# Gate and up of the feed-forward: four pairs of k-tiles of a block in seven block products for eight, and two k-tiles' residues by an accumulating DMA

## The chip, the cores and the metric

The kernel runs on one core of a Trainium2 chip. The metric is the time of one execution in device microseconds (us), the median of several runs. The core has a tensor engine (PE, with PEld for its weight loads), a vector engine (DVE), a scalar engine (ACT), GpSimd (POOL), and SyncE (SP), which here issues loads and stores. Each engine takes its own instructions in their written order.

## The reference

One residual block on 256 tokens of 2048 values, in fp32:

```python
h  = x + W_out @ [DiffAttn(xn) ; ConformerConv(xn)]     # xn = rms_norm(x) * norm1_g
hn = rms_norm(h) * norm2_g
out = h + (silu(hn @ w_gate) * (hn @ w_up)) @ w_down    # 2048 -> 5632 -> 2048
```

The change concerns the two products hn @ w_gate and hn @ w_up. Together they are 2 x 256 x 2048 x 5632 multiplications, the largest part of the block.

## The kernel before, in words

Every product with a weight keeps fp32's precision by a split: each operand is rounded to a shorter form (hi), and the residue (lo = value - hi) is kept beside it. A product is three matrix products, hi x hi, lo x hi and hi x lo, summed in PSUM. The activations' hi and lo (xhi, hhi, ahi and xlo, hlo, alo) are made once. The weights arrive in fp32 and are split as they come.

The unit of this stream is a chunk: two k-tiles of 128 rows by 512 columns of a weight, half a megabyte. `split_chunk` (L265) issues its load into `raw` (SP), has ACT round it into `whi` (L275) and DVE subtract to get `wlo` (L276). `multiply` (L289) issues the first half of its PE work, the eight products with whi (L306, L307), then the second half, the four with wlo (L312): 2 k-tiles x 2 halves of the tokens x 3 = 12 products of 128x128 by 128x512. `run_chunks` emits the split of a chunk AHEAD = 2 chunks before its products. raw has RAW_BUFS = 5 buffers, whi and wlo HL_BUFS = 4 each, so that ACT's rounding waits until PE has used an earlier chunk's whi.

Beside this stream run generators (`silu_done`, `up_done`, `out_done` and others): after each half of a chunk, `resume` lets each go on to its next `yield`, and what it emits there stands in the engines' queues at that place. Since each engine works in order, this emission order is the schedule. DVE's convolution and other filler are fed in by `run_side`.

Stages in order: the products with w_in with attention and convolution (to about 265 us), w_out (to about 360 us), then the feed-forward. Its 5632 columns are 11 blocks j of 512. For each, a gate sum (16 k-tiles, 8 chunks) and an up sum (8 chunks) for both halves of the tokens, in two of the four PSUM banks `acc` each; then silu of the gate on ACT (L713), a = up x rstd x silu on DVE (L721), four transposes on PE twice (L729), and the split of the result (L732 ACT, L733 DVE). FGROUPS = (6, 5): after six blocks, and after the last five, a pass of w_down over the blocks so far adds into h (L746, DVE). hT holds the transpose of h x norm2_g as hi and lo; the row factor rstd2 is applied only in L713 and L721.

A block has 16 chunks, 192 products and 16 transposes.

Of the kernel before, what the change touches and what calls it, by code (L numbers as in the profile page):

```python
# [38 lines left out]
# where the rows of the gains and biases begin, 128 values to a row  # L39
# [41 lines left out]
def tile_block(  # L81
# [9 lines left out]
    lhs = ctx.enter_context(tc.tile_pool(name="lhs", bufs=KD))  # L91
# [7 lines left out]
    # ---------------------------------------------------------------- inputs and constants  # L99
# [7 lines left out]
    # the tensor engine's clock rises while the first loads are under way  # L107
# [7 lines left out]
    rows = const.tile([NR, P], F32, tag="rows", name="rows")  # L115
    act.dma_start(out=rows, in_=gains)
    # a first use of the activation table before anything waits for it
# [11 lines left out]
    cw = const.tile([P, NCT, W], F32, tag="cw", name="cw")  # L129
# [15 lines left out]
    def late_constants():  # L145
# [10 lines left out]
        # q is scaled by 1/sqrt(d) through its gain  # L156
        act.mul(gb[:, 0, :], gb[:, 0, :], 1.0 / math.sqrt(DH))
        hd = DH // 2
        for i, key in enumerate("qk"):
            for m in range(NM):  # L160
                t = const.tile([P, 2, DH], F32, tag=f"gcs{key}{m}", name=f"gcs{key}{m}")
# [12 lines left out]
    def negative_lambda():  # L174
        """-lambda = exp(l2) - exp(l1) - lambda_init"""
# [5 lines left out]
    def rsqrt_mean(dst, ss, n, eps):  # L181
        """dst = (ss / n + eps) ** -0.5 on a few columns."""
# [4 lines left out]

    def lhs_pair(pfx, k):
        hi = lhs.tile([P, S], F32R, tag="lhi", name=f"{pfx}hi{k}")
        lo = lhs.tile([P, S], F32R, tag="llo", name=f"{pfx}lo{k}")  # L190
        return hi, lo

    def split_scaled(pair, src, scale):
        """hi + lo = src * scale, src in PSUM."""
# [21 lines left out]
    # banks of the aux pool that are read in a later stage than they are written  # L216
# [7 lines left out]
    # work of the vector engine that fills what the stream leaves free  # L224
# [12 lines left out]
    def side_step():  # L237
        """One step of the two oldest chains by turns: a step waits for the one before it."""
# [11 lines left out]
    def block(w, cols, ks, xs, done=None, bkey=None, first=True, last=True, spare=False, cuts=()):  # L250
        """Products of the k-tiles ks with columns of w, summed in two banks."""
# [6 lines left out]
        while i < len(ks):  # L258
# [4 lines left out]
                               done=done if i == len(ks) else None, spare=spare))  # L263

    def split_chunk(w, k0, nk, cols, width, **_):  # L265
        view = lambda t: t.rearrange("p (k n) -> p k n", n=width)[:, :nk]
        raw = view(wp.tile([P, NK * N], F32, tag="raw", name="raw", bufs=RAW_BUFS))
        o = 0
        for c, n in cols:
            sp.dma_start(out=raw[:, :, o : o + n],  # L270
                         in_=w[k0 * P : (k0 + nk) * P, c : c + n].rearrange("(k p) n -> p k n", p=P))
            o += n
        hi = view(wp.tile([P, NK * N], F32R, tag="whi", name="whi", bufs=HL_BUFS))
        lo = view(wp.tile([P, NK * N], F32R, tag="wlo", name="wlo", bufs=HL_BUFS))
        act.copy(hi, raw)  # L275
        dve.tensor_tensor(lo, raw, hi.bitcast(F32), ALU.subtract)  # L276
        spend(LO_US * nk * width / N)
        return hi, lo
# [10 lines left out]
    def multiply(c, hi, lo):  # L289
# [24 lines left out]
        if c is chunks[-1]:  # L314
            # one half of the tokens after the other, which shortens the end
# [18 lines left out]
    def run_chunks():  # L334
        ready = deque()
        n = len(chunks)
        i = 0
        for t in range(n):
            while i < min(n, t + 1 + lead(t)):
                if i in before:  # L340
                    before[i]()
                ready.append(split_chunk(**chunks[i]))
                i += 1
            multiply(chunks[t], *ready.popleft())
# [3 lines left out]
    # ---------------------------------------------------------------- x, its transpose  # L348
# [40 lines left out]
    # ---------------------------------------------------------------- convolution channels  # L389
# [7 lines left out]
    def glu_done(c0, nct, ps):  # L397
        """ps holds the gates of nct channel tiles, then what they gate."""
# [40 lines left out]
    # layer norm with tokens on partitions, and back  # L439
# [5 lines left out]
    def conv_back(b):  # L445
# [21 lines left out]
        # the table of the silu below, ahead of need  # L467
# [34 lines left out]
    # ---------------------------------------------------------------- attention  # L502
# [19 lines left out]
    def qk_rows(key, b, m, ps):  # L522
        """Norm and rotation of the heads of block b, and their transpose."""
# [32 lines left out]
    def attend_scores(hd):  # L556
# [63 lines left out]
        # in the place of the head's q, which is done with  # L620
# [48 lines left out]
    # ---------------------------------------------------------------- output projection  # L669
# [4 lines left out]
    def out_done(n, ps):  # L674
# [18 lines left out]
        if n == D // N - 1:  # L693
# [8 lines left out]
            ffn["pool"] = ctx.enter_context(tc.tile_pool(name="ffn", bufs=1))  # L702

    # ---------------------------------------------------------------- feed-forward
# [4 lines left out]
    def silu_done(ps):  # L709
        yield  # L710
        for m in range(NM):
            sil[m] = ffn["pool"].tile([P, N], F32, tag="sil", name="sil", bufs=4)
            act.activation(sil[m], ps[m], AF.Silu, scale=rstd2[m])  # L713

    def up_done(j, ps):
# [3 lines left out]
        for m in range(NM):  # L719
            a = fp.tile([P, N], F32, tag="a", name="a", bufs=4)  # L720
            dve.scalar_tensor_tensor(a, ps[m], rstd2[m], sil[m], ALU.mult, ALU.mult)  # L721
            aa.append(a)
        yield
        for t in range(N // P // 2):
# [5 lines left out]
            hi = fp.tile([P, 2, S], F32R, tag="ahi", name="ahi", bufs=FGROUPS[0] * 2)  # L730
            lo = fp.tile([P, 2, S], F32R, tag="alo", name="alo", bufs=FGROUPS[0] * 2)
            act.copy(hi, pt)  # L732
            dve.tensor_tensor(lo, pt, hi.bitcast(F32), ALU.subtract)  # L733
            for i in range(2):
                actT[j * (N // P) + 2 * t + i] = (hi[:, i, :], lo[:, i, :])
            yield

# [13 lines left out]
    # ---------------------------------------------------------------- the order of it all  # L751
# [19 lines left out]
    for g, nb in enumerate(FGROUPS):  # L771
        for j in range(j0, j0 + nb):
            block(w_gate, j * N, range(KD), fh, silu_done)
# [5 lines left out]
    lead = lambda t: 1 if t < len(XPARTS) else AHEAD  # L779
# [30 lines left out]
```

## Time and profile before

| What | Value |
|---|---|
| runs before | 1091.35, 1090.16, 1091.2 us; median 1091.2 |
| span of the profiled execution | 1089.8 us (its own time beside the span is not listed; the median is 1.4 above the span) |
| one feed-forward block (403.50 to 447.97 us) | 44.47 us |
| granted clock of TensorE, mean | 0.998 |

A row of the groups gives the line, the engine and the operation, what is written and read, the shapes and the number of instructions; behind the first bar the busy time in us and the mean ns of one; behind the second the idle time of the engine just before them and what ended it. A row of the timeline gives the start, the duration, the engine, the line and the operation, and in brackets the idle time before it. A row of the waits gives who waited for whom, the total in us, the number of times and the longest. The window rows are explained where they stand.

### The profile page before, as it was taken

The numbers are of one execution on the slowest core, as the hardware profiler recorded it, in microseconds if no ns is written. First come the engines' busy times: TensorE is split into PE (matmuls) and PEld (weight loads), VectorE is DVE, ScalarE is ACT, GpSimd is POOL, SyncE is SP. The second block draws the span as 40 slices with busy tenths as digits, with TensorE's granted clock in tenths as the row PEclk, the third lists the DMA queues.
The fourth block names the chain that finished last, engine by engine and source line by source line (L and its number), as shares of the span: only waits on it lengthen the run. The fifth ranks groups of instructions, "written<-read, shape, count | busy, mean of one in ns | idle before, by whom it ended". The sixth has DMA issues, their size and how long they took to land.

```text
span 1089.8 us, 13224 instructions
## 1 busy us (share of the span) xinstructions
PE 1079.0 (99%) x4952; PEld 894.0 (82%) x4952; DVE 647.1 (59%) x828; ACT 509.6 (47%) x719; POOL 49.1 (5%) x77
## 2 busy tenths in 40 slices
PE   8999999999999999999999999999999999999998
PEld 7988888877888888888888888888888888888886
DVE  4799989898766544544545454444454454544443
ACT  6644566755754544434444343333443444433332
POOL 0030112210100100000000000000000000000000
PEclk9999999999999999999999999999999999999999
DMA  8756665554456557666575555556666656653654
GB/s 241 233 177 198 190 189 161 154 169 155 155 181 206 174 172 220 187 192 189 168 214 184 192 192 193 192 187 190 194 186 192 189 169 211 186 192 108 219 204 146
DMA packets 118733, 203.02 MB, mean 186 GB/s; under 512 B 6932, under 2 KB 28878, under 8 KB 118668
## 3 DMA queue, kind: packets, MB, share of 16 engines
q1 hardware_dynamic: 118608, 202.14, 59.7%
q8 instruction: 39, 0.64, 0.2%
q14 instruction: 26, 0.21, 0.1%
q10 hardware_dynamic: 60, 0.03, 0.0%
HBM read 200.04 MB, written 2.10 MB: 185 GB/s over the span
## 4 chain that ended last, share of the span: by engine, by line
PE 92%; DVE 3%; ACT 2%; POOL 1%; issue 1%; DMA 1%; SPq 1%; DVEq 0%; ACTq 0%
PE acc L307 30%; PE acc L312 30%; PE acc L306 30%; DVE y L431 1%; DVE wlo L276 1%; PE ps_a L729 1%; ACT whi L275 1%; DMA h<-in_x_dram 1%; PE ps_o L643 1%; ACT junk L355 0%; POOL rsq L185 0%; PE ps_h L686 0%; SPq L360 0%; POOL fq L186 0%; SPq L270 0%
## 5 line engine op out<-in xcount | busy, mean ns | idle before, releaser
L276 DVE TENSOR_TENSOR wlo<-raw,whi 128x1024 fp32r<-128x1024 f32 (+1 forms) x377 | 456.4, 1221 | 337.3 <-ACT whi L275 304.5
L275 ACT CAST whi<-raw 128x1024 fp32r<-128x1024 f32 (+1 forms) x377 | 390.8, 1051 | 366.4 <-PE acc L307 326.6
L306 PE MATMUL acc<-whi,hhi 128*128 128x512 f32 x704 | 274.8, 390 | 0.0
L307 PE MATMUL acc<-whi,hlo 128*128 128x512 f32 x704 | 274.1, 389 | 0.0
L312 PE MATMUL acc<-wlo,hhi 128*128 128x512 f32 x704 | 189.2, 391 | 0.0
L307 PEld LDWEIGHTS acc<-whi,hlo 128*128 128x128 f32 x704 | 132.2, 188 | 27.3
L306 PEld LDWEIGHTS acc<-whi,hhi 128*128 128x128 f32 x704 | 132.2, 188 | 27.2
L312 PEld LDWEIGHTS acc<-wlo,hhi 128*128 128x128 f32 x704 | 131.4, 188 | 26.8
L306 PE MATMUL acc<-whi,ahi 128*128 128x512 f32 x384 | 150.7, 392 | 0.0
L307 PE MATMUL acc<-whi,alo 128*128 128x512 f32 x384 | 150.5, 392 | 0.0
L306 PE MATMUL acc<-whi,xhi 128*128 128x512 f32 (+1 forms) x352 | 130.0, 376 | 2.8 <-ACT xhi L196 2.8
L307 PE MATMUL acc<-whi,xlo 128*128 128x512 f32 (+1 forms) x352 | 128.6, 372 | 0.5 <-DVE xlo L197 0.4
L431 DVE SCALAR_TENSOR_TENSOR y<-upad,cw,y 128x256 f32<-128x256 f32 x240 | 103.6, 481 | 3.5 <-ACT y L424 3.0
L312 PE MATMUL acc<-wlo,ahi 128*128 128x512 f32 x384 | 103.6, 391 | 0.0
L312 PE MATMUL acc<-wlo,xhi 128*128 128x512 f32 (+1 forms) x352 | 88.7, 377 | 1.4 <-DVE wlo L276 1.2
L306 PEld LDWEIGHTS acc<-whi,ahi 128*128 128x128 f32 x384 | 72.1, 188 | 15.9
L307 PEld LDWEIGHTS acc<-whi,alo 128*128 128x128 f32 x384 | 72.1, 188 | 15.3
L312 PEld LDWEIGHTS acc<-wlo,ahi 128*128 128x128 f32 x384 | 71.9, 188 | 15.6
L306 PEld LDWEIGHTS acc<-whi,xhi 128*128 128x128 f32 x352 | 66.5, 189 | 14.7 <-ACT xhi L196 3.2
L307 PEld LDWEIGHTS acc<-whi,xlo 128*128 128x128 f32 x352 | 66.6, 189 | 11.9 <-DVE xlo L197 0.9
L312 PEld LDWEIGHTS acc<-wlo,xhi 128*128 128x128 f32 x352 | 62.3, 190 | 13.0 <-DVE wlo L276 2.2
L733 DVE TENSOR_TENSOR alo<-ps_a,ahi 128x512 fp32r<-128x512 f32 x22 | 15.2, 691 | 46.0 <-ACT ahi L732 46.0
(138 smaller groups left out, 544.2 us busy)
## 6 DMA issues: line engine op xcount, KB each, us to landing
raw<-in_w_gate_dram SPq DMA_DIRECT2D x88, 512.0 KB, 4.4
raw<-in_w_up_dram SPq DMA_DIRECT2D x88, 512.0 KB, 4.5
raw<-in_w_down_dram SPq DMA_DIRECT2D x88, 512.0 KB, 4.2
raw<-in_w_in_dram SPq DMA_DIRECT2D x48, 512.0 KB, 3.7
raw<-in_w_out_dram SPq DMA_DIRECT2D x32, 512.0 KB, 3.7
raw<-in_w_in_dram SPq DMA_DIRECT2D x62, 256.0 KB, 3.6
h<-in_x_dram SPq DMA_DIRECT2D x6, 256.0 KB, 6.1
out_dram<-h SPq DMA_DIRECT2D x6, 256.0 KB, 2.5
```

The lines of the kernel that those rows point to most:

```text
L275: act.copy(hi, raw)
L276: dve.tensor_tensor(lo, raw, hi.bitcast(F32), ALU.subtract)
L306: pe.matmul(ps[m], xhi[:, ms], hi[:, j, :], start=c["first"] and j == 0, stop=False)
L307: pe.matmul(ps[m], xlo[:, ms], hi[:, j, :], start=False, stop=False)
L312: pe.matmul(ps[m], xhi[:, ms], lo[:, j, :], start=False, stop=c["last"] and j == nk - 1)
L431: dve.scalar_tensor_tensor(y[:, ct, :], src, wk, y[:, ct, :], ALU.mult, ALU.add)
L643: pe.matmul(o[:, m, :], wT[:, (0 if m == 0 else 1 + k), :], v_sb[k][:, hd * E : (hd + 1) * E], start=k == 0, stop=k == m)
L729: pe.transpose(pt[:, i, m * P : (m + 1) * P], aa[m][:, c : c + P], ident)
L733: dve.tensor_tensor(lo, pt, hi.bitcast(F32), ALU.subtract)
```

## The change

Blocks 1 to 10 are computed by `fast_block`. The 16 k-tiles of a block form 8 pairs (k, k + 8). For the first NS = 4 pairs, up and gate, both k-tiles and both halves of the tokens make a 2 x 2 by 2 x 2 product of blocks, done with seven block products in place of eight (Winograd's form). A unit of kind "s" is one pair: `load_pair` gets its 1 MB by two DMAs (tile wb), `round_pair` makes four combinations of the weights on DVE (tile wt, L860 to L862) and rounds all seven operands on ACT (tile wh, L863 and L864), `split_pair` makes the seven residues on DVE (tile wl, L868 and L869), and `multiply_pair` (L878) issues 7 x 3 = 21 products into seven of the eight PSUM banks, which all hold sums now. The other eight k-tiles go as chunks of 12 products, kinds "g" and "u" (`multiply_two`, L894), so a block is 4 x 21 + 8 x 12 = 180 products. The units of a block stand in the order "sggsggsuusuu".

For one chunk of each of gate and up (k-tiles 14 and 15) wlo is not made by DVE: ACT writes -hi into wlo (L302) and POOL issues a DMA that adds raw to it (L303), 512 KB, 20 in all.

The seven sums become gate and up by `products_done` after the fourth pair (one ACT copy, six DVE additions L947 to L953, two silu) and by `block_done` after the block (two additions L964, two multiplications L967); the transposes and alo (L776) follow as before. Here the row factor has to be in the operand: `make_forms` (L786), which runs beside the products of block 0, multiplies hn by it, forms the seven combinations of the activations and splits them. It takes 32 DVE operations of 256 elements, 11 of 512 and 2 of 1024, ACT roundings and two plain fp32 products (L797). Block 0 stays in the plain form.

Besides: HL_BUFS is 3 and RAW_BUFS 4; FGROUPS is (4, 4, 3), so a w_down pass comes before blocks 4 and 8 and at the end; in a changed block ACT's rounding runs three units ahead and DVE's residues two; hi and lo of the activations are allocated in pairs; some constants move to a pool that is freed before the feed-forward; a is read by L761, h is added to in L979, and the plain chunk's lines are L299 (whi), L308 (wlo), L338, L339 and L344 (products). Comments are removed.

```diff
-RAW_BUFS = 5
+RAW_BUFS = 4
-HL_BUFS = 4
+HL_BUFS = 3
-FGROUPS = (6, 5)
+FGROUPS = (4, 4, 3)
+HK = KD // 2
+NS = 4
+REST = [k for k in range(KD) if k % HK >= NS]
+TWOS = [tuple(REST[i : i + 2]) for i in range(0, len(REST), 2)]
+BY_DMA = TWOS[-1:]
+ORDER = "sggsggsuusuu"
+Q1, Q6, Q7, Q5, Q2, Q4, Q3, QX = range(8)
+PRODUCTS = ((Q1, 0, 5), (Q6, 5, 1), (Q7, 6, 2), (Q5, 4, 3), (Q2, 1, 6), (Q4, 3, 0), (Q3, 2, 4))
+HI_AHEAD, LO_AHEAD = 3, 2
...
+    def round_chunk(c):
+        c["hi"] = c["view"](wp.tile([P, NK * N], F32R, tag="whi", name="whi", bufs=HL_BUFS))
+        act.copy(c["hi"], c["raw"])
+        if c["by_dma"]:
+            c["lo"] = c["view"](wp.tile([P, NK * N], F32R, tag="wlo", name="wlo", bufs=HL_BUFS))
+            act.activation(c["lo"], c["raw"], AF.Copy, scale=-1.0)
+            pool.dma_start(out=c["lo"], in_=c["raw"].bitcast(F32R), accum_op=ALU.add)
...
+            hi_lead, lo_lead = lead(t)
+            while i < min(n, t + 1 + hi_lead):
+                chunks[i]["load"](chunks[i])
+                chunks[i]["round"](chunks[i])
+                i += 1
+                if hi_lead == lo_lead:
+                    chunks[j]["split"](chunks[j])
+                    j += 1
+            while j < min(n, t + 1 + lo_lead):
+                chunks[j]["split"](chunks[j])
+                j += 1
+            chunks[t]["multiply"](chunks[t])
...
+    def make_forms():
...
+        ps = aux_ps.tile([P, N], F32, tag="aux", name="ps_r")
+        for m in range(NM):
+            pe.matmul(ps[:, m * P : (m + 1) * P], ones, diag[:, m * P : (m + 1) * P], start=True, stop=True)
...
+        for k in range(KD):
+            while k not in hT:
+                yield
+            t = hn[k // HK][:, k % HK, :]
+            hi, lo = hT[k]
+            dve.tensor_tensor(t, hi.bitcast(F32), lo.bitcast(F32), ALU.add)
+            dve.tensor_tensor(t, t, rb, ALU.mult)
+            if k % 4 == 3:
+                yield
...
+        dve.scalar_tensor_tensor(f[:, 4], a21, -1.0, a22, ALU.mult, ALU.subtract)
+        dve.scalar_tensor_tensor(f[:, 5], f[:, 4], -1.0, a11, ALU.mult, ALU.subtract)
+        dve.tensor_tensor(f[:, 6], a11, a21, ALU.subtract)
+        dve.tensor_tensor(f[:, 2], a12, f[:, 5], ALU.subtract)
...
+    def round_pair(c):
...
+        dve.tensor_tensor(t[:, 2:4], b[:, 1:3], b[:, 0:1].to_broadcast([P, 2, N]), ALU.subtract)
+        dve.tensor_tensor(t[:, 1], b[:, 1], t[:, 3], ALU.add)
+        dve.tensor_tensor(t[:, 0], t[:, 1], b[:, 3], ALU.subtract)
+        act.copy(c["hi"][:, 4:], b[:, 1:])
+        act.copy(c["hi"][:, :4], t)
+
+    def split_pair(c):
+        c["lo"] = ffn["pool"].tile([P, 7, N], F32R, tag="wl", name="wl", bufs=2)
+        dve.tensor_tensor(c["lo"][:, 4:], c["b"][:, 1:], c["hi"][:, 4:].bitcast(F32), ALU.subtract)
+        dve.tensor_tensor(c["lo"][:, :4], c["t"], c["hi"][:, :4].bitcast(F32), ALU.subtract)
...
+    def multiply_pair(c):
...
+        for n, (q, f, w) in enumerate(PRODUCTS):
+            ps = sum_bank(c, q)
+            first, last = c["first"].get(q), c["last"].get(q)
+            pe.matmul(ps, fhi[:, f, p, :], c["hi"][:, w], start=bool(first), stop=False)
+            pe.matmul(ps, flo[:, f, p, :], c["hi"][:, w], start=False, stop=False)
+            pe.matmul(ps, fhi[:, f, p, :], c["lo"][:, w], start=False, stop=bool(last))
+            if n in (1, 3, 5):
+                resume()
...
+    def products_done(q):
...
+        act.copy(w1, q[Q1])
+        yield
+        yield
+        dve.tensor_tensor(u2, q[Q6], w1, ALU.add)
+        dve.tensor_tensor(u3, q[Q7], u2, ALU.add)
+        dve.tensor_tensor(w4, q[Q5], u3, ALU.add)
+        dve.tensor_tensor(u2, q[Q5], u2, ALU.add)
+        yield
+        dve.tensor_tensor(w1, q[Q2], w1, ALU.add)
+        dve.tensor_tensor(u3, q[Q4], u3, ALU.add)
+        act.activation(w1, w1, AF.Silu)
+        act.activation(u3, u3, AF.Silu)
...
+        for m, i in enumerate((Q3, QX)):
+            dve.tensor_tensor(u[m], q[i], u[m], ALU.add)
+        yield
+        for m in range(NM):
+            dve.tensor_tensor(u[m], u[m], g[m], ALU.mult)
```

How the instructions stand on the engines, at the places of which the prediction speaks. First DVE at the start of the first feed-forward block behind a w_down pass. The kernel before, the end of the pass (L746 adds the sums into h) and the gate chunks that follow:

```order
L746 TENSOR_TENSOR h_78<-h_78,acc 128x512
L746 TENSOR_TENSOR h_79<-h_79,acc 128x512
L276 TENSOR_TENSOR wlo<-raw,whi 128x1024 x12
L746 TENSOR_TENSOR h_78<-h_78,acc 128x512
L746 TENSOR_TENSOR h_79<-h_79,acc 128x512
L276 TENSOR_TENSOR wlo<-raw,whi 128x1024 x16
```

The changed kernel, the same place before block 4; the pair's wt and wl are L860 to L869, and the h addition is L979:

```order
L308 TENSOR_TENSOR wlo<-raw,whi 128x1024 x5
L860 TENSOR_TENSOR wt<-wb 128x1024
L861 TENSOR_TENSOR wt<-wb,wt 128x512
L862 TENSOR_TENSOR wt<-wt,wb 128x512
L868 TENSOR_TENSOR wl<-wb,wh 128x1536
L869 TENSOR_TENSOR wl<-wt,wh 128x2048
L308 TENSOR_TENSOR wlo<-raw,whi 128x1024
L860 TENSOR_TENSOR wt<-wb 128x1024
L861 TENSOR_TENSOR wt<-wb,wt 128x512
L862 TENSOR_TENSOR wt<-wt,wb 128x512
L308 TENSOR_TENSOR wlo<-raw,whi 128x1024
L979 TENSOR_TENSOR h_78<-h_78,acc 128x512
```

The last of the five wlo is that of the pass's last chunk. Between it and the addition that frees the first of that pass's two banks there stand now the whole preparation of the first pair, the first part of the next pair's, and two wlo; before, three wlo stood there.

PE at this place, the kernel before (with the engines that an instruction waits for in brackets): the last products of w_down and the first of the gate.

```order
L312 MATMUL acc<-wlo,ahi 128x512 [waits DVE_49]
L312 MATMUL acc<-wlo,ahi 128x512 x3
L306 MATMUL acc<-whi,hhi_3220 128x512 [waits Activation_49]
L307 MATMUL acc<-whi,hlo_3221 128x512
L306 MATMUL acc<-whi,hhi_3220 128x512
```

The changed kernel, where each q is a bank of sums:

```order
L344 MATMUL acc<-wlo,ahi_5031 128x512 x3
L885 MATMUL q_5578<-wh,fhi 128x512 [waits Activation_49]
L886 MATMUL q_5578<-wh,flo 128x512
L887 MATMUL q_5578<-wl,fhi 128x512 [waits DVE_49]
L885 MATMUL q_5582<-wh,fhi 128x512 [waits Activation_49]
L886 MATMUL q_5582<-wh,flo 128x512
L887 MATMUL q_5582<-wl,fhi 128x512 [waits DVE_49]
L885 MATMUL q_5588<-wh,fhi 128x512 [waits DVE_49]
L886 MATMUL q_5588<-wh,flo 128x512
L887 MATMUL q_5588<-wl,fhi 128x512
L885 MATMUL q_5592<-wh,fhi 128x512 [waits DVE_49]
```

The third bank, q_5588, and the fourth, q_5592, are those of the last w_down sums, and their first product waits for DVE.

Last, DVE in block 0 (gate). The kernel before has there, behind the two reductions that end rstd2, only wlo; in the changed kernel stands the end of make_forms between them:

```order
L817 SCALAR_TENSOR_TENSOR sums<-hn 128x512
L818 SCALAR_TENSOR_TENSOR sums<-sums,hn 128x512
L819 TENSOR_TENSOR sums<-hn 128x512
L820 TENSOR_TENSOR sums<-hn,sums 128x512
L308 TENSOR_TENSOR wlo<-raw,whi 128x1024
L828 TENSOR_TENSOR flo<-hn,fhi 128x512 x2
L829 SCALAR_TENSOR_TENSOR flo<-hn,fhi 128x512
L832 TENSOR_TENSOR flo<-sums,fhi 128x512 x4
L308 TENSOR_TENSOR wlo<-raw,whi 128x1024
L842 TENSOR_TENSOR clo<-hn,chi 128x1024 x2
L308 TENSOR_TENSOR wlo<-raw,whi 128x1024 x4
```

Before these rows stand the 32 operations of L808 and L809 (eight, a wlo, sixteen, a wlo, eight).

More of the change, by code (lines that the diff above doesn't have):

```diff
@@ new lines, in multiply_pair @@
+    def multiply_pair(c):
+        while "hi" not in forms:
+            resume()
+        fhi, flo, p = forms["hi"], forms["lo"], c["k"]
+        for n, (q, f, w) in enumerate(PRODUCTS):
[5 more added lines that the diff above has]
+            if n in (1, 3, 5):
+                resume()
+        resume()
+        if c["done"]:
+            start(c["done"](c["sums"]))
@@ new lines, in multiply_two @@
+    def multiply_two(c):
+        hi, lo = c["hi"], c["lo"]
+        qs = (Q3, QX) if c["kind"] == "u" else (Q2, Q4)
+        for i, k in enumerate(c["ks"]):
+            x1, x2 = forms["plain"][k]
+            for m, q in enumerate(qs):
+                ms = slice(m * P, (m + 1) * P)
+                ps = sum_bank(c, q)
+                pe.matmul(ps, x1[:, ms], hi[:, i, :], start=i == 0 and bool(c["first"].get(q)), stop=False)
+                pe.matmul(ps, x2[:, ms], hi[:, i, :], start=False, stop=False)
+        resume()
+        for m, q in enumerate(qs):
+            ms = slice(m * P, (m + 1) * P)
+            for i, k in enumerate(c["ks"]):
+                pe.matmul(sum_bank(c, q), forms["plain"][k][0][:, ms], lo[:, i, :], start=False,
+                          stop=i == 1 and bool(c["last"].get(q)))
+        resume()
+        if c["done"]:
+            start(c["done"](c["sums"]))
@@ L738, in down_done, with block_done @@
+    def block_done(j, q):
+        while "g" not in halfway:
+            yield
+        g, u = halfway.pop("g"), halfway.pop("u")
+        yield
+        for m, i in enumerate((Q3, QX)):
+            dve.tensor_tensor(u[m], q[i], u[m], ALU.add)
+        yield
+        for m in range(NM):
+            dve.tensor_tensor(u[m], u[m], g[m], ALU.mult)
+        yield
+        yield from transposed(j, u)
     def down_done(g, n, ps):
```

156 lines of the change are left out of this document (124 added, 32 removed).

## The prediction

> **What bounds the kernel now.** I read the page first, for the engines' shares.
>
> ```profile
> span 1089.8 us, 13224 instructions
> PE 1079.0 (99%) x4952; PEld 894.0 (82%) x4952; DVE 647.1 (59%) x828; ACT 509.6 (47%) x719; POOL 49.1 (5%) x77
> ```
>
> TensorE is busy for 99% of the span. Then the table by windows, over one feed-forward block (gate and up of one j, between two ends of an up sum), and the timeline for two ends of one chunk. The window's columns are the length, then the busy time of PE, PEld, DVE, ACT and POOL, the granted clock, the DMA share and GB/s.
>
> ```profile
> 403.50:447.97 44.47, 44.47 (x202) 36.83 (x201) 22.03 (x20) 18.88 (x20) 0.00 (x0) 1.00 0.64 190
> ...
> 500.93 1.07 PE L312 MATMUL acc<-wlo,hhi 128*128 128x512 f32 x4
> ...
> 503.65 1.07 PE L312 MATMUL acc<-wlo,hhi 128*128 128x512 f32 x4
> ```
>
> PE never stops in it. A chunk of 12 products takes 503.65 - 500.93 = 2.72 us, so one product takes 0.2267, and the 192 of a block 43.5; the transposes make up the rest. DVE has only 22.03 us of work there. The chain of waits says who waits for whom, and the timeline shows one chunk's preparation.
>
> ```profile
> ACT whi L275 <- PE acc L307: 326.6, 206, 1.7
> DVE wlo L276 <- ACT whi L275: 304.5, 216, 6.9
> ...
> 561.92 1.05 ACT L275 CAST whi<-raw 128x1024 fp32r<-128x1024 f32 x1 [1.67 <-PE acc L307]
> ...
> 563.00 1.23 DVE L276 TENSOR_TENSOR wlo<-raw,whi 128x1024 fp32r<-128x1024 f32 x1 [1.49 <-ACT whi L275]
> ```
>
> ACT and DVE wait for PE to free a whi or wlo, never the other way round: PE bounds every block, with ACT and DVE a fixed lead ahead of it. A change here is worth what it takes from PE, less what DVE then makes PE wait.
>
> **The change part by part.** *Products.* A changed block has 4 x 21 + 8 x 12 = 180 products for 192. Ten blocks: 10 x 12 x 0.2267 = **-27.2**. The two plain fp32 products of L797 (128x128) are new; the nearest row is the transposes' of that size, 272 ns each.
>
> ```profile
> L729 PE MATMUL ps_a<-ident,a 128*128 128x128 f32 x88 | 13.2, 272 | 0.0
> ```
>
> Two make **+0.5**. All transposes stay.
>
> *DVE's prices.* Spacing, not busy time, is what a full queue pays.
>
> ```profile
> 200.03 1.22 DVE L276 TENSOR_TENSOR wlo<-raw,whi 128x1024 fp32r<-128x1024 f32 x1
> 201.17 0.48 DVE L431 SCALAR_TENSOR_TENSOR y<-upad,cw,y 128x256 f32<-128x256 f32 x1
> ...
> 221.06 0.41 DVE L544 TENSOR_TENSOR t<-qn,gcsq 128x256 f32<-128x256 f32 x1
> ...
> 221.50 0.69 DVE L545 TENSOR_TENSOR t<-t,t 128x512 f32<-128x512 f32 x1
> ...
> 222.11 1.27 DVE L431 SCALAR_TENSOR_TENSOR y<-upad,cw,y 128x256 f32<-128x256 f32 x3
> ...
> L746 DVE TENSOR_TENSOR h<-h,acc 128x512 f32<-128x512 f32 x14 | 9.0, 684 | 6.2 <-PE acc L312 6.2
> ...
> L733 DVE TENSOR_TENSOR alo<-ps_a,ahi 128x512 fp32r<-128x512 f32 x22 | 15.2, 691 | 46.0 <-ACT ahi L732 46.0
> ```
>
> From start to start: 1024 elements 1.14 us, 512 take 0.61, so 1536 take 1.67 and 2048 take 2.20 on that line, and 256 about 0.38 (0.34 on the line, 0.41 busy when the next depends on it). With PSUM operands 0.65. A pair costs wt 1.22 + 0.69 + 0.69 = 2.6 (each depends on the one before) and wl 1.67 + 2.20 = 3.9, so 6.5. Per block: 4 x 6.5 + 6 wlo x 1.14 + 12 x 0.65 (six sums, four of block_done, two alo) = 40.6 us, for 180 x 0.2267 + 0.95 = 41.8 of PE. DVE goes from 50% to 97% of a block: it keeps up on average, and whatever it owes PE at one spot it cannot catch up. ACT has 4 x 3.6 of pairs, 10 x 1.05 and some 3 us, 28 us: no bound.
>
> *Forms (L786), once in block 0.* DVE gets 32 x 0.38 + 11 x 0.61 + 2 x 1.14 = 21.2 us of it between the wlo of its chunks. Count from the end of the fifth gate chunk. DVE can start the forms at 1.35 (behind wlo of chunk 7) and stands, by its order, eight of them, a wlo, sixteen, a wlo, eight and the four sums, a wlo: 1.35 + 3.1 + 1.14 + 6.2 + 1.14 + 3.1 + 2.6 + 1.14 = 19.8, where chunk 10 (its first half done at 0.5 + 5 x 2.72 + 1.81 = 15.9) wants that wlo: 3.9 of waiting. Then seven flo (4.3) and a wlo, done at 25.3; chunk 11 has had its first half by 22.4: 2.9. Two clo and a wlo, 28.7, for 28.0: 0.7. Together **+7.5** (bounds 0, if the lead were larger than two chunks, and 21).
>
> *Starts out of the plain form (blocks 1, 4, 8).* The third product of a block's first pair takes the bank which the h additions (L979) or a (L761) read. These stand in DVE's queue behind wlo of the last chunk, wt and wl of the pair, a wlo, wt of the next pair, a wlo. With three wlo buffers the first of these may start three chunks before T, the end of the last plain sum: T - 8.16. It adds 1.14 + 2.6, then wl's two, the second of them after ACT's 2.1 us of rounding wt: -8.16 + 3.74 + 2.1 + 2.2 = T - 0.1; a wlo, a wt and a wlo make T + 4.8, and one addition T + 5.4. PE comes to that product at T + 6 x 0.2267 = T + 1.4. Three times 4.0 = **+12.0**. In the kernel before, the same addition has but wlo ahead of it, and another bank is taken first.
>
> *From block to block (seven times).* The six sums start 0.6 after the fourth pair's end A (ACT's copy first), six chained at 0.69 end at A + 4.8; the block ends at A + 5.44 = T. Then wt of the next block's second pair (2.6), a wlo, and four of block_done: T + 5.8. PE wants the transposes behind its first pair, T + 21 x 0.2267 = T + 4.8. Seven times 1.0 = **+7.0**.
>
> *Clock.* PE's longest wait in the profile, at its start, and what followed:
>
> ```profile
> 12.60:15.10 2.50, 0.06 (x1) 0.00 (x0) 1.22 (x1) 2.47 (x7) 0.00 (x0) 1.00 1.13 329
> ...
> 17.00:20.40 3.40, 3.40 (x18) 3.40 (x18) 2.56 (x5) 3.29 (x10) 0.00 (x0) 0.51 1.14 258
> ```
>
> After 2.5 us of nothing PE had half its clock for 3.4 us, which costs 1.7. The change adds five waits over 2.5 us. I take two of the five, **+3.4**, since the row is from a stretch where PE had done little before; bounds 0 and 8.5. [...]
>
> *Fewer buffers.* raw 5 to 4 and whi, wlo 4 to 3 bind outside the feed-forward too. In the q, k, v stage PE already has no lead:
>
> ```profile
> 223.30 1.22 DVE L276 TENSOR_TENSOR wlo<-raw,whi 128x1024 fp32r<-128x1024 f32 x1
> ...
> 224.57 1.20 PE L312 MATMUL acc<-wlo,xhi 128*128 128x512 f32 x4 [1.23 <-DVE wlo L276]
> ```
>
> There DVE's other work sets the lateness, not a buffer, so I take **+0.7**; bounds 0 and 11 (22 chunks in 60 us, half a microsecond each).
>
> *Accumulating DMA (L303).* It replaces a wlo on DVE, and is counted so above. By ACT's and PE's order it must land 10.9 us after its issue. No DMA of POOL is in the trace; the nearest row is a load of the same 512 KB.
>
> ```profile
> raw<-in_w_gate_dram SPq DMA_DIRECT2D x88, 512.0 KB, 4.4
> ```
>
> Reading two operands might double it, 8.8: still hidden. I take 0; the upper bound is a rival. [...]
>
> *At nothing:* FGROUPS in three groups adds eight h additions (0.65 each, beside plain products where DVE is half idle); lhs in pairs changes no instruction; the last pass ends as before.
>
> **Sum.** -27.2 + 0.5 + 7.5 + 12.0 + 7.0 + 3.4 + 0.7 = +3.9 on the span of 1089.8, so 1093.7; the runs' median is 1.4 above that span, so **1095.1**.
>
> **The rivals.** *The block starts do not wait (faster).* Place: DVE's queue at the three starts and the seven seams. It decides if the first addition is ready by T + 1.4, that is if DVE is 4.0 us further on, and block_done 1.0. For it: DVE idles half of the plain block before, so its queue might run ahead where I hold it back for a buffer. Against it: that buffer is freed by PE alone, and the row at 561.92 shows that ACT starts only when PE lets it. Price: -12.0 - 7.0 and 1.7 of clock, 1074.4. Half of that gone gives about 1085.
>
> *The accumulating DMA lands late (slower).* Each microsecond over 10.9 is met 20 times by PE: landing at 14 us gives 20 x 3.1 = 62, and 1157. For it: nothing like it was measured here. Against: 4.4 us for the same bytes.
>
> *The q, k, v stage loses its lead (slower).* Up to 11 us by the bound above, so 1098 to 1106. For it: the wait at 224.57. Against: the wait is for DVE's filler.
>
> *That it does not save the products* is ruled out by the order, where a block's rows count 180.
>
> **How the numbers follow.** Forecast case 0.55 (1088 to 1105, of which 0.10 fall within 2.2 us of 1091.2, 0.2%, which is about what a measurement of this kernel can tell from no change; 0.02 below and the rest above). Starts that do not wait 0.29, all of it faster (1068 to 1086). Late DMA 0.07, q, k, v 0.09, slower both. Faster 0.31, same 0.10, slower 0.59. The range leaves out the late DMA and the lower half of the faster rival: 1076 to 1110.
>
> **What would show it.** PE's busy time should fall by about 26 us and its share to 96 or 97%; DVE should be near 97% busy in a window of a changed block, and such a block 42.8 us from end to end. At the start of blocks 1, 4 and 8 the product L885 of the third bank should wait about 4 us for L761 or L979, at the seven seams the transposes for L967 about 1 us, and in block 0 L344 for wlo L308 about 7 us in three waits. The forecast is wrong if these waits are under half, if a changed block takes PE's 41.8 or clearly more than 43, if the DMAs of L303 take over 10 us, or if the stage from 197 to 258 us has grown.

## The result, and the profile after

The changed kernel takes 1117.4 us (median of 1115.92 to 1122.97) against 1091.3 before: a ratio of 1.0248, interval 1.022 to 1.0276. That is 26 us slower, where 3.9 were forecast and 1110 was the upper end. The profiled execution is the longest of the four, with a span of 1121.2 us; the others have 1114.1 to 1117.0. Its page:

```profile
span 1121.2 us, 13273 instructions
PE 1074.2 (96%) x4836; PEld 877.5 (78%) x4836; DVE 852.4 (76%) x1061; ACT 588.4 (52%) x761; POOL 61.4 (5%) x98
```

PE has 116 matrix instructions fewer and is busy for only 5 us less. The waits of PE say where DVE holds it up:

```profile
PE q L885 <- DVE h L979: 8.6, 2, 4.3
PE ps_a L772 <- DVE sum L967: 7.9, 20, 1.2
PE acc L344 <- DVE wlo L308: 6.7, 5, 3.8
PE acc L338 <- ACT whi L299: 6.1, 4, 2.1
PE q L885 <- DVE a L761: 5.0, 1, 5.0
PE q L885 <- DVE sum L964: 3.4, 7, 0.5
```

The windows, by stage: block 0; the first changed block; one that follows another; and the last w_down pass without its end. The number right behind the busy times of the five engines is the granted clock.

```profile
353.02:406.30 53.28, 47.75 (x205) 37.89 (x204) 45.31 (x72) 28.43 (x39) 2.62 (x5) 0.97 0.53 176
406.30:456.93 50.63, 45.20 (x190) 36.23 (x188) 41.44 (x38) 25.99 (x24) 1.98 (x2) 0.93 0.68 216
456.93:500.79 43.86, 42.87 (x190) 34.45 (x188) 40.10 (x39) 25.96 (x24) 1.76 (x2) 1.00 0.70 217
1039.14:1117.21 78.07, 70.99 (x297) 56.69 (x295) 37.36 (x41) 24.53 (x26) 0.00 (x0) 0.96 0.44 148
```

The same stretches of the kernel before:

```profile
353.90:398.34 44.44, 44.44 (x201) 36.82 (x200) 22.28 (x25) 21.28 (x27) 3.89 (x4) 1.00 0.63 189
974.82:1085.76 110.94, 110.94 (x489) 90.74 (x487) 52.22 (x49) 39.15 (x39) 0.00 (x0) 1.00 0.49 171
```

Set side by side by stage, from the first and last products of each in the two traces (us):

| Stage | before | after | difference |
|---|---|---|---|
| up to the first gate product | 353.9 | 353.0 | -0.9 |
| block 0 | 44.4 | 53.3 | +8.8 |
| blocks 1 to 10 | 443.7 | 453.1 | +9.3 |
| w_down passes (two before, three after; 88 chunks in both) | 243.7 | 257.9 | +14.2 |

A changed block that follows another takes 43.86 us and saves 0.6, not 2.7. The w_down passes, which the prediction had at nothing, lose most. The four differences are the whole of the two spans' 31.4 us.

### The profile page after: what moved, and what is told of

Same layout as the page of the kernel before. It is cut to its first block, busy times and chain, and to the rows that moved or that the text cites. A ratio compares the mean times of both kernels' runs of the same rounds, so it can differ in the third digit from the quotient of the medians.

```text
span 1121.2 us, 13273 instructions
## 1 busy us (share of the span) xinstructions
PE 1074.2 (96%) x4836; PEld 877.5 (78%) x4836; DVE 852.4 (76%) x1061; ACT 588.4 (52%) x761; POOL 61.4 (5%) x98
## 4 chain that ended last, share of the span: by engine, by line
PE 76%; DVE 13%; DMA 4%; issue 4%; ACT 2%; POOL 1%; SPq 0%; DVEq 0%; ACTq 0%; POOLq 0%
PE acc L338 14%; PE acc L339 14%; PE acc L344 14%; PE q L902 5%; PE q L908 5%; PE q L903 5%; PE q L885 5%; PE q L887 5%; PE q L886 5%; DVE wlo L308 4%; DMA raw<-in_w_down_dram 2%; ACT whi L299 1%; DVE wt L860 1%; PE ps_a L772 1%; DMA raw<-in_w_in_dram 1%
## 5 line engine op out<-in xcount | busy, mean ns | idle before, releaser
L308 DVE TENSOR_TENSOR wlo<-raw,whi 128x1024 fp32r<-128x1024 f32 (+1 forms) x277 | 336.8, 1220 | 211.2 <-ACT whi L299 177.6
L299 ACT CAST whi<-raw 128x1024 fp32r<-128x1024 f32 (+1 forms) x297 | 310.2, 1049 | 299.4 <-PE acc L339 148.3
L338 PE MATMUL acc<-whi,ahi 128*128 128x512 f32 x384 | 151.2, 394 | 5.6 <-ACT whi L299 5.6
L339 PE MATMUL acc<-whi,alo 128*128 128x512 f32 x384 | 150.6, 392 | 0.0
L338 PE MATMUL acc<-whi,xhi 128*128 128x512 f32 (+1 forms) x352 | 130.3, 376 | 2.8 <-ACT xhi L216 2.3
L885 PE MATMUL q<-wh,fhi 128*128 128x512 f32 x280 | 113.6, 406 | 17.0 <-DVE h L979 8.6
L339 PE MATMUL acc<-whi,xlo 128*128 128x512 f32 (+1 forms) x352 | 128.9, 372 | 0.5 <-DVE xlo L217 0.4
L902 PE MATMUL q<-whi,chi 128*128 128x512 f32 x320 | 126.3, 395 | 0.0
L903 PE MATMUL q<-whi,clo 128*128 128x512 f32 x320 | 125.4, 392 | 0.0
L887 PE MATMUL q<-wl,fhi 128*128 128x512 f32 x280 | 112.0, 400 | 0.4 <-DVE wl L869 0.4
L886 PE MATMUL q<-wh,flo 128*128 128x512 f32 x280 | 111.5, 398 | 0.0
L864 ACT CAST wh<-wt 128x2048 fp32r<-128x2048 f32 x40 | 76.5, 1913 | 61.7 <-DVE wt L862 61.6
L344 PE MATMUL acc<-wlo,ahi 128*128 128x512 f32 x384 | 104.9, 395 | 0.0
L869 DVE TENSOR_TENSOR wl<-wt,wh 128x2048 fp32r<-128x2048 f32 x40 | 91.5, 2289 | 6.2 <-ACT wh L864 6.2
L338 PEld LDWEIGHTS acc<-whi,ahi 128*128 128x128 f32 x384 | 72.7, 189 | 22.0 <-ACT whi L299 6.9
L344 PE MATMUL acc<-wlo,xhi 128*128 128x512 f32 (+1 forms) x352 | 88.2, 376 | 1.2 <-DVE wlo L308 1.2
L908 PE MATMUL q<-wlo,chi 128*128 128x512 f32 x320 | 87.0, 394 | 0.0
L344 PEld LDWEIGHTS acc<-wlo,ahi 128*128 128x128 f32 x384 | 72.9, 191 | 15.2
L339 PEld LDWEIGHTS acc<-whi,alo 128*128 128x128 f32 x384 | 72.7, 189 | 15.1
L338 PEld LDWEIGHTS acc<-whi,xhi 128*128 128x128 f32 x352 | 66.7, 190 | 14.5 <-ACT xhi L216 2.7
```

What stands on the lines that cost most here:

```text
L299: act.copy(c["hi"], c["raw"])
L308: dve.tensor_tensor(c["lo"], c["raw"], c["hi"].bitcast(F32), ALU.subtract)
L338: pe.matmul(ps[m], xhi[:, ms], hi[:, j, :], start=c["first"] and j == 0, stop=False)
L339: pe.matmul(ps[m], xlo[:, ms], hi[:, j, :], start=False, stop=False)
L344: pe.matmul(ps[m], xhi[:, ms], lo[:, j, :], start=False, stop=c["last"] and j == nk - 1)
L885: pe.matmul(ps, fhi[:, f, p, :], c["hi"][:, w], start=bool(first), stop=False)
```

## The experiments

Theory A is the prediction's mechanism: PE waits for where an addition, a form or a load stands in another engine's queue, and for the half clock behind such a wait. Its rivals: the units are slow in themselves or DVE's load is too high, so that a wait which is taken away comes back; or the fewer buffers cost time everywhere.

**Buffers alone, in the kernel before.**

```diff
-RAW_BUFS = 5
+RAW_BUFS = 4
```

> The kernel before with four raw buffers for five, nothing else. Theory A (the buffer that the change takes away is what hid the loads behind the stores of the last w_down pass): the three stretches where ACT waits 8 to 9 us for a load of w_down make PE wait some 2 to 3 us each, so 6 to 11 us slower, all of it in the last pass. Rival (the buffer costs nothing, as the prediction had it, and the last pass is slow for another reason): within 2 us of 1091.

1091.3 us, ratio 1.000 (0.999 to 1.0009). The raw buffer costs nothing, and theory A's first guess for the last pass is wrong.

```diff
-HL_BUFS = 4
+HL_BUFS = 3
```

> The kernel before with three buffers of whi and wlo for four, nothing else. Theory A: the lead of ACT and DVE over PE falls by one chunk and still covers the plain chunks, so within 3 us of 1091. Rival (the shorter lead itself costs time in every stage): 5 us or more slower.

1095.0, ratio 1.0035 (1.0023 to 1.0047): between the two expectations. The trace puts all of it in the last pass, 115.69 us for 110.94. DVE and SP in it, with the last pass's h addition and its stores:

```profile
1031.98 1.28 DVE L746 TENSOR_TENSOR h<-h,acc 128x512 f32<-128x512 f32 x2
...
1032.69 0.95 SPq L748 DMA_DIRECT2D out_dram<-h  x2
...
PE acc L306 <- ACT whi L275: 3.9, 3, 1.8
```

In the kernel before the addition waited for PE alone:

```profile
1030.41 1.28 DVE L746 TENSOR_TENSOR h<-h,acc 128x512 f32<-128x512 f32 x2 [0.89 <-PE acc L312]
```

With three buffers the wlo that stands ahead of the addition in DVE's queue waits, through ACT's rounding, for PE, so the addition no longer starts at the sum's end but when that wlo is made: here at 1031.98, for 1030.41 in the kernel before. The store behind it in SP's queue goes out as much later (1032.69 for 1031.12), and the loads of w_down stand behind the store (1033.74 for 1032.17). The changed kernel has both smaller counts and a last group of three blocks; the two counts together were not run in the kernel before.

**Stores on another queue, in the changed kernel.**

```diff
-                    sp.dma_start(out=out[m * P : (m + 1) * P, hs], in_=h[m][:, hs])
+                    pool.dma_start(out=out[m * P : (m + 1) * P, hs], in_=h[m][:, hs])
```

> The changed kernel, with the stores of the result issued by POOL, so that no load of w_down stands behind a store in SP's queue. Theory A: the last pass goes from 82 to about 72 us, so 8 to 11 us faster, about 1108. Rival (the last pass is slow because its loads are slow, or for want of a buffer alone): within 3 us of 1117.

1113.1, ratio 1.0206 (1.0189 to 1.0223), some 4 us faster. In the changed kernel the chain addition, store, load, rounding, product reads:

```profile
1059.85 1.28 DVE L979 TENSOR_TENSOR h<-h,acc 128x512 f32<-128x512 f32 x2
...
1060.55 0.95 SPq L981 DMA_DIRECT2D out_dram<-h  x2
...
1066.99 1.04 ACT L299 CAST whi<-raw 128x1024 fp32r<-128x1024 f32 x1 [8.32 <-DMA raw<-in_w_down_dram]
...
1068.09 0.50 PE L338 MATMUL acc<-whi,ahi 128*128 128x512 f32 x1 [1.45 <-ACT whi L299]
```

With the stores on POOL the pass has the full clock, and PE idles in it for 1.46 us where it idled for 7.08:

```profile
1037.44:1105.74 68.30, 66.84 (x297) 54.62 (x295) 37.35 (x41) 24.61 (x26) 3.82 (x7) 1.00 0.52 170
```

The pass goes from 78.07 (72.6 and 74.2 in traces of variants that leave it alone) to 68.30, and the end behind it, with the last stores on POOL, from 4.0 to 5.5. The direction is theory A's; the size, 4 for 8 to 11, is smaller, since the profiled execution's 78 us, with two stretches of half clock in it, is more than the pass takes in the other traces.

**The additions first, at the three starts.** Before a changed block that follows a plain sum emits its next pair, the generators are resumed; the transposes behind block 0's up sum are put off by as many resumptions (not shown).

```diff
+EARLY = 2
...
+            if "kind" in chunks[t] and "kind" not in chunks[t - 1]:
+                for _ in range(EARLY):
+                    resume()
             hi_lead, lo_lead = lead(t)
```

> The changed kernel, where the additions that free the banks of a plain sum (h, or a) are emitted ahead of the next pair's combinations, at the three starts of changed blocks only. Theory A (PE waits for the place of these in DVE's queue, and then runs at half clock): the waits of 5.0 and twice 4.3 us fall under 1, and the half clock behind them goes, so 14 to 19 us faster, 1098 to 1103. Rival (the units are slow by themselves, from contention, and the waits would come back elsewhere): under 6 us faster.

1100.2, ratio 1.0092 (1.0074 to 1.0111): 17 us faster, as theory A has it. Blocks 1 and 4:

```profile
406.21:450.01 43.80, 42.50 (x189) 34.46 (x188) 40.77 (x38) 25.28 (x23) 1.98 (x2) 1.00 0.79 243
627.63:669.77 42.14, 41.58 (x181) 33.71 (x180) 38.67 (x36) 23.48 (x20) 1.76 (x2) 1.00 0.77 234
```

They took 50.63 and 47.44 us, and the clock is 1.00 for 0.93 and 0.96. No operation was removed.

**The additions first at all seams.** The same for each block's end, with EARLY = 3 and the transposes two products later.

```diff
-            if "kind" in chunks[t] and "kind" not in chunks[t - 1]:
+            if t and ("kind" in chunks[t] or "kind" in chunks[t - 1]) and chunks[t - 1]["done"] and chunks[t - 1].get("kind") != "s":
```

> The changed kernel, where at every block's end the additions (h, a, and block_done's four) are emitted ahead of the next unit's combinations; the transposes come two products later. Theory A (waits by place in DVE's order): besides the 17 us of the three starts, the seven changed blocks of 43.86 us that follow another go to about 42.2, and the w_down passes lose about 1 each: 28 to 32 us faster than the changed kernel, about 1087, and faster than the kernel before. Rival (DVE, 40 us of a block busy, is the bound, so a wait taken from one place comes back at the residues of the next pair): blocks stay above 43 and the time above 1093.

1090.8, ratio 0.9994 (0.9984 to 1.0005): 26.6 us faster than the changed kernel, and the same as the kernel before, where theory A had hoped for 4 us better.

```profile
450.60:493.39 42.79, 42.41 (x189) 34.50 (x188) 40.10 (x39) 25.63 (x24) 1.76 (x2) 1.00 0.70 209
```

A block is 42.79, not the 42.2 expected; PE still waits for DVE's alo, 2.6 us in all. The rival, that DVE's load would bring the waits back, falls: DVE has the same 40.10 us in a block that is 1.07 shorter.

**Forms early.** The sixteen additions hi + lo go ahead of the row factor, and the sixteen multiplications become four of 1024 elements.

```diff
+        for k in range(KD):
+            hi, lo = hT[k]
+            dve.tensor_tensor(hn[k // HK][:, k % HK, :], hi.bitcast(F32), lo.bitcast(F32), ALU.add)
...
+        for k in range(0, KD, 4):
+            t = hn[k // HK][:, k % HK : k % HK + 4, :]
+            dve.tensor_tensor(t, t, rb.to_broadcast([P, 4, S]), ALU.mult)
+            yield
```

> The changed kernel, where the sixteen additions of the forms are emitted before the row factor is known, in a stretch where DVE idles, and the sixteen multiplications are four of 1024 elements. Theory A: DVE is about 8 us further on in block 0, PE's waits there go from 8 us to about 3 and the half clock behind them with them: block 0 falls from 53.3 to 47 to 49 us, 4 to 6 us faster, about 1112. Rival (block 0 is long because of ACT's roundings or of loads): under 2 us faster.

1112.2, ratio 1.0192 (1.0176 to 1.0207), 5 us faster. Block 0 goes from 53.28 to 47.84, with the full clock:

```profile
353.28:401.12 47.84, 45.84 (x206) 36.99 (x204) 43.59 (x60) 29.01 (x40) 2.77 (x5) 1.00 0.62 198
```

**No accumulating DMA.**

```diff
-BY_DMA = TWOS[-1:]
+BY_DMA = []
```

> The changed kernel without accumulating DMAs: DVE makes all residues, 2.3 us more per changed block. Theory A (DVE's load is under PE's on average, its place in the order counts): 42.4 of 43.9 us, so 0 to 6 us slower, 1117 to 1123. Rival 1 (DVE is the bound): a block goes to 46, 20 us slower. Rival 2 (the DMA's landing of 6 us or ACT's added work holds PE up): faster by 3 us or more.

1110.3, ratio 1.0178 (1.0161 to 1.0195): 7 us faster, though DVE has 2.3 us more to do per block. That is the second rival's direction: the accumulation costs more than the DVE work that it spares. Two neighbouring blocks, 42.16 and 43.27 us for 43.86:

```profile
680.23:722.39 42.16, 42.16 (x190) 34.58 (x189) 40.31 (x39) 22.28 (x21) 0.00 (x0) 1.00 0.63 200
722.39:765.66 43.27, 42.76 (x190) 34.45 (x188) 42.10 (x41) 24.06 (x22) 0.00 (x0) 1.00 0.62 194
```

**Two chunks more by DMA.**

```diff
-BY_DMA = TWOS[-1:]
+BY_DMA = TWOS[-2:]
```

> The changed kernel with the residues of four k-tiles in place of two by accumulating DMA, 40 in all. Theory A1 (each DMA holds a raw buffer for its 6 us, and late loads make DVE wait more than the 1.1 us that it is spared): 4 us or more slower than 1117. Rival (the DMA itself is harmless and what made the kernel without it faster was the ACT operation ahead of the sums' copy): the same direction, under 2 us; if DVE's load were what counts: faster.

1116.8 (1111.0 to 1120.8), ratio 1.0246 (1.0214 to 1.0278): no different from the changed kernel. Theory A1, that each DMA costs by holding its raw buffer, finds no support. Nor does the theory that ACT's added work costs the time by itself, since that is doubled here. The DMAs are no longer all hidden: in the trace PE waits for a landing six times, 3.1 us in all.

**ACT's part without the DMA.** ACT writes -hi into wlo, then DVE makes the residue over it.

```diff
-            pool.dma_start(out=c["lo"], in_=c["raw"].bitcast(F32R), accum_op=ALU.add)
```

> The changed kernel where ACT still writes -hi into wlo for the two chunks, but DVE then makes the residue over it and no accumulating DMA is issued. It parts the two things that the kernel without accumulation took away at once. If the DMA (its landing, the raw buffer that it holds) cost the 7 us: about 1110. If ACT's operation, 1.05 us ahead of the next pair's roundings, cost them: 1117 or more.

1126.2, ratio 1.0329 (1.0305 to 1.0354). A block takes 44.60:

```profile
500.19:544.79 44.60, 42.88 (x190) 34.45 (x188) 35.59 (x34) 23.54 (x22) 0.00 (x0) 1.00 0.37 121
```

So taking away the DMA alone does not bring the 7 us: without it, but with ACT's operation, the kernel is slower still. In this variant DVE's residue also stands behind ACT's write of the same wlo, and what else ACT's early write changes is told below, in the account of the prediction.

**The place of the stationary operands.**

```diff
-    lhs = ctx.enter_context(tc.tile_pool(name="lhs", bufs=KD // 2))
     wp = ctx.enter_context(tc.tile_pool(name="wp", bufs=4))
+    lhs = ctx.enter_context(tc.tile_pool(name="lhs", bufs=KD // 2))
```

> The changed kernel, with the pool of the stationary operands of the plain products (lhs) allocated behind the pool of the weights, 40 KB further up in each partition; no instruction changes. A chunk of twelve products takes 2.72 us where its stationary operand lies in that pool, and 2.745 to 2.755 where it lies in the pool ffn, in both kernels. If the place in memory sets the rate, plain chunks may go to 2.745 and the time to 1119 to 1122. If not: 2.72 and 1117 within 2 us.

1118.4, ratio 1.0249 (1.0229 to 1.027): the same. Moving this pool up by 40 KB does not slow the kernel; why the products of the pool ffn are slower (2.74 and 2.75 us a chunk for 2.72) stays open.

**Three edits together.** Seams, forms, and POOL for the stores of the first three columns.

```diff
-                    sp.dma_start(out=out[m * P : (m + 1) * P, hs], in_=h[m][:, hs])
+                    (sp if parts == 2 else pool).dma_start(out=out[m * P : (m + 1) * P, hs], in_=h[m][:, hs])
```

> The changed kernel with three edits together: additions first at all seams, forms early, and the stores of the first three columns of the last pass issued by POOL (the last column's stay on SP). Theory A, whose costs add up because they lie in different stretches: 27 (seams and starts) + 5 (forms) + 4 to 6 (stores) = 36 to 38 us faster than the changed kernel, 1079 to 1082, and 9 to 12 us faster than the kernel before. Rival (DVE's load gives part of it back, the gains overlap): 1086 or more.

1079.3, ratio 0.9889 (0.9874 to 0.9903): 38 us faster than the changed kernel and 1.1% faster than the kernel before. The gains add up. One block, and the last pass:

```profile
446.48:489.25 42.77, 42.38 (x189) 34.50 (x188) 40.11 (x39) 25.63 (x24) 1.76 (x2) 1.00 0.71 220
1007.26:1074.20 66.94, 66.67 (x297) 54.60 (x295) 37.17 (x41) 24.60 (x26) 3.32 (x6) 1.00 0.53 173
```

**The fourth edit, no accumulation.** `BY_DMA = []` besides.

> As the one with three edits, and without accumulating DMAs. Theory A1 (the DMA holds its raw buffer until it has landed, so the loads behind it are issued late, and DVE then waits for a rounding; that cost 7 us in the changed kernel): 2 to 7 us faster than with three edits. Rival (with the seams mended DVE's 42.4 us per block is now more than PE's 42.1, so its load decides): 0 to 5 us slower than with three edits.

1082.3, ratio 0.9916 (0.9901 to 0.993): 3 us slower than with three edits, as the rival had it. With the seams mended, blocks go from 42.77 to as much as 43.95, and PE waits more for DVE's alo (L781 in these kernels). First with three edits, then with four:

```profile
PE ps_a L777 <- DVE alo L781: 2.6, 7, 0.4
...
PE ps_a L777 <- DVE alo L781: 7.0, 5, 1.5
```

That fits the rival, by which DVE's load now decides. The same operation that cost 7 us in the one order is worth 3 in the other.

## Why the prediction was wrong

The sign was right, and so were most of the places where PE waits; four steps failed. Block 0 came out as summed (7.5 + 0.5 for the forms, 8.8 measured), by luck in part, as its half clock made up for shorter waits. Blocks 1 to 10 were to gain 27.2 less 12.0, 7.0 and 3.4, which leaves 4.8, and they lost 9.3; the w_down passes were at nothing and lost 14.2. Some 14 us are missing in each, nearly all of the 27.5 between the sum, +3.9, and this execution's +31.4; between the medians it is 22.

- **Products, -27.2.** The price was wrong. Ends of two neighbouring chunks of a changed block, in the trace after:

```profile
453.26 1.08 PE L908 MATMUL q<-wlo,chi 128*128 128x512 f32 x4
456.01 1.08 PE L908 MATMUL q<-wlo,chi 128*128 128x512 f32 x4
```

  2.75 us a chunk, not 2.72; twenty-four products average 0.2296, so a block of 180 costs 41.3 and saves 2.2, ten of them 22. The warning stood in the trace of before, in a w_down pass (first fence below), whose chunks took 2.74. That kernel's ahi, like the changed kernel's forms, lies in the pool ffn. The changed kernel keeps ahi in the pool lhs, and there w_down runs at 2.72 (second fence below), which gives some 2 us back (88 chunks).

```profile
703.09 1.07 PE L312 MATMUL acc<-wlo,ahi 128*128 128x512 f32 x4
705.83 1.07 PE L312 MATMUL acc<-wlo,ahi 128*128 128x512 f32 x4
```

```profile
1054.70 1.07 PE L344 MATMUL acc<-wlo,ahi 128*128 128x512 f32 x4
1057.42 1.07 PE L344 MATMUL acc<-wlo,ahi 128*128 128x512 f32 x4
```

- **"At nothing: the last pass ends as before."** This is the largest single step in this execution. The pass was looked at for what its order changed, not for what its buffers did. Three whi and wlo make the addition late (in the trace after, the sum's end is 0.9 behind the last row of the fence above, at 1058.3, and the addition starts at 1059.85), the store later, the loads later still, and PE waits. Of the 6.1 us of PE's waits for whi above, 5.6 lie in this pass. Against the 66.94 of the version with three edits, whose additions also come first, the pass costs 11 us here and 6 in the shortest trace of a variant that leaves it alone; by the medians, the stores on POOL give 4 of them back. "Fewer buffers, +0.7" looked for the loss in the q, k, v stage, and the stages up to the feed-forward lost nothing (353.0 for 353.9).

- **Clock, +3.4.** Four waits of 3.8 to 5.0 us, and at each the half clock, from the wait's last part on or right behind it. Here are its stretches, whole: one in block 0, three at the starts, two in the last pass.

```profile
388.17:391.58 3.41, 3.25 (x8) 2.50 (x9) 3.41 (x7) 3.41 (x5) 0.00 (x0) 0.50 0.50 154
412.06:418.88 6.82, 5.34 (x13) 4.07 (x14) 2.08 (x3) 1.56 (x1) 0.00 (x0) 0.50 0.30 96
640.75:644.16 3.41, 3.41 (x10) 2.67 (x9) 3.41 (x3) 0.73 (x1) 0.00 (x0) 0.50 0.60 174
906.99:913.81 6.82, 4.49 (x11) 3.52 (x12) 6.74 (x6) 2.85 (x2) 0.00 (x0) 0.50 0.52 166
1087.90:1091.31 3.41, 3.41 (x9) 2.64 (x8) 2.65 (x3) 2.34 (x3) 0.00 (x0) 0.50 0.71 249
1108.38:1111.79 3.41, 3.41 (x9) 2.67 (x8) 2.45 (x2) 1.12 (x2) 0.00 (x0) 0.50 0.03 7
```

  Four of four, where the sum took two of five, and two of them twice as long as the row that set the price. In the last pass the half clock came 1.0 and 1.2 us behind the ends of waits of 2.15 and 2.03 us, and none came behind one of 1.45. PE is busy for 23.3 of these 27.3 us, and a product takes 0.43 us from start to start in them, for 0.23 outside; an estimate from that is that 10.8 is lost, where the sum had 3.4. Taken with the waits, the three starts cost 50.63 + 47.44 + 47.90 less the 43.80 + 42.14 + 42.11 without them: 17.9 us, for 12.0 and a part of the 3.4. The row at the start of the old trace, with 2.5 us of waiting and 3.4 us at a clock of 0.51, was a better guide than the choice of two of five.

- **Accumulating DMA at nothing; "ACT: no bound".** The DMA did land hidden, as forecast, at 6.2 us in the median:

```profile
wlo<-raw POOLq DMA_DIRECT2D x20, 512.0 KB, 6.2
```

  That lies between the 4.4 of the load that the prediction went by and its double. The step that failed is "it replaces a wlo on DVE, and is counted so above": the sum spared DVE 20 wlo and left out that the accumulated one takes its buffer earlier. ACT writes it (L302) three units ahead, while DVE makes the wlo of the chunk before only two ahead. So ACT's comes first in the turn of the three wlo buffers, and DVE's has to wait until PE is through with one chunk more. A chunk's last products in the trace after, and DVE and ACT behind their end:

```profile
486.80 1.08 PE L908 MATMUL q<-wlo,chi 128*128 128x512 f32 x4
...
487.98 1.23 DVE L308 TENSOR_TENSOR wlo<-raw,whi 128x1024 fp32r<-128x1024 f32 x1 [1.96 <-issue]
...
488.00 1.06 ACT L302 ACTIVATE wlo<-raw 128x1024 fp32r<-128x1024 f32 x1
...
DVE wlo L308 <- issue: 31.5, 12, 4.2
```

  The same place without accumulation, where DVE does not wait:

```profile
708.26 1.22 DVE L308 TENSOR_TENSOR wlo<-raw,whi 128x1024 fp32r<-128x1024 f32 x1
...
708.40 1.08 PE L908 MATMUL q<-wlo,chi 128*128 128x512 f32 x4
```

  The profile names no releaser ("issue"), but each of the twelve waits ends 0.1 us behind a chunk's last wlo product. They take 31.5 us from DVE, where the 20 wlo spare it 20 x 1.14 = 22.8. Without accumulation there is no such wait; in the variant with ACT's write and no DMA there are 25.9 us of them, and DVE's work besides; with three edits there are 7.0, and there the accumulation pays (1079.3 for 1082.3). DVE's lateness is met by PE at the seams, so these 7 us are no item beside the seams' 7.0 but lie in the same waits: in the shorter of the two blocks above, 42.16 us, PE is busy throughout. That the buffer is the reason is read from the order and the traces; a kernel with a fourth wlo buffer, which would test it alone, was not run.

What held: the starts wait 5.0 and twice 4.3 us for L761 and L979 (forecast 4.0); PE idles 53.28 - 47.75 = 5.5 us in block 0 for the forms (forecast 7.5), and with the half clock there the block is 8.8 longer; the seams cost 1.07 each by experiment (forecast 1.0). Behind them PE waits another 0.5 each for the sums of L964, 3.4 in all, and the w_down passes lose some 1.4 each at their transposes; neither was in the sum. DVE's 40.6 us a block was 40.10, and with the additions first it kept up. Of the signs that the prediction named, two came: a changed block took 43.86, clearly more than 43, and PE's busy time fell by 5 us, not 26. The rival with waits that do not come about was refuted by the waits themselves, and its price of 1074 was too low: the version with the additions first at all seams takes these waits away and needs 1090.8. The 1079.3 of the three edits has the forms and the stores mended too, which the rival did not count.

## What to carry to other kernels

Before an in-order engine is loaded to 97%, go through the places where another engine waits for one small operation of it, and emit that operation ahead of bulk work: here that alone was worth 27 us and turned a loss of 26 into none. Price an added wait of some 4 us with the slow clock behind it (here 3.4 or 6.8 us at 0.50), and follow a smaller buffer count through every stage, above all through those where loads queue behind stores. An operation that relieves one engine is priced by who waits where for the engine that takes it over, and for the buffers that it takes earlier: the same accumulating DMA cost 7 us before the order was mended and saved 3 after.

## What the runs showed of the hardware

The rate of a product went with the pool that holds its stationary operand, with the same instruction and shapes, in both kernels: 0.2267 us from the pool lhs (chunks of 2.72 us, hhi before and ahi after), 0.2288 on average over two chunks from the pool ffn before (ahi) and 0.2296 after (chi). A shift of the pool lhs by 40 KB changed nothing (1118.4 for 1117.4), so whether the place itself is the cause is open.

In the changed kernel's trace PE has four waits of 3.7 us or more (3.78, 5.03, 4.28 and 4.29), and at each of them the granted clock was 0.50, for 3.41 or 6.82 us; a product then took 0.43 us from start to start, for 0.23. The variants without accumulation, with two chunks more by DMA and with ACT's part alone have four such waits each (3.72 to 5.02 us), and behind all twelve of them there are products 0.42 to 0.43 us apart. In the feed-forward of these four kernels the same was seen behind the three waits between 2.0 and 2.5 us (2.15 and 2.03 in the changed kernel, 2.43 with ACT's part alone); once, with ACT's part alone, it was seen from 962.5 us on with no wait over 1.21 us in the 40 us before. Behind the twelve waits between 1.4 and 2.0 us there and in the feed-forward of the kernels with three and four edits it was not seen.

The accumulating DMA of 512 KB from one buffer on the chip into another landed after 6.2 us in the median of the 20 in the changed kernel's trace.
